# One kernel, four edits: moves of turned tiles issued by GpSimd, softmax weights turned right behind the softmax, shared buffers, and the last heads' results turned on TensorE

## The chip, the core and the metric

The kernel runs on one core of one Trainium2 chip. A core has five engines with instruction queues of their own: TensorE (PE: matrix products), VectorE (DVE), ScalarE (ACT), GpSimd (POOL) and SyncE (SP, which here only issues transfers). Each takes its instructions strictly in the order in which they stand; semaphores make one wait for another. Transfers (DMAs) are put into queues by SyncE or GpSimd and run on 16 DMA engines beside everything else. Matrix results land in PSUM, everything else lives in SBUF, both with 128 partitions.

The metric is the device time of the program in microseconds; the median of three runs before is 928.0 (927.65, 928.0 and 930.58). TensorE's clock has two levels, 2.4 and 1.2 GHz; the profile gives the granted clock of a stretch as a share of full speed.

## What is computed

A trunk of two pre-norm layers over 256 tokens of width 2048, everything in float32, weights read from HBM:

```
layer 0:  u = rms_norm(x);  [qa ka va qb kb vb gate] = u @ w_in_even        # 2048 -> 6656
  A: 8 heads of 128, 2 kv heads; q, k RMS-normalised and rotated
     ya = softmax(qa ka^T / sqrt(128)) va
  B: 8 heads; two maps of 64 each, with a linear bias on the distance
     p  = softmax(s1) - lam * softmax(s2);   yb = rms_norm(p vb) * (1 - lambda_init)
  h = x + (concat(ya, yb) * silu(gate)) @ w_out_even                          # 16 heads -> 2048
layer 1:  u = rms_norm(h);  [q k v gate] = u @ w_in_odd                       # 2048 -> 8192
  C: 16 heads of 128, three dilated windows merged into one masked, biased softmax
     h = h + (softmax(...) v * silu(gate)) @ w_out_odd
out = rms_norm(h)
```

## The kernel before

**Products.** Each float32 weight is split into a high and a low part (`hi`, `lo`), likewise each activation, and three matmuls give one product (`mm3`, lines 156 to 158). Weights come in pieces of 128 x 1024 (512 KB): `wgroup` (line 132) loads one on SyncE's queue (line 146) into one of three `raw` buffers, ScalarE makes `hi` (line 148), VectorE `lo` (line 149). A *group* below is what TensorE does with one piece: 12 matmuls of 512 columns. A projection of 512 columns (`job_t`, line 173) has eight groups. Two PSUM banks of the pool `acc` hold a job; four are there.

**Order of the work.** A scheduler works out the order of the whole program from program order, which gives priorities, and its own estimates of times. It also decides which groups of a later job fill the time in which TensorE would wait for heads. In program order the even layer has, for each of two halves g (lines 527 to 549): the queries of A, the gate, four A heads (`softmax_a`, `weighted_v`), the gate and the queries and keys of B, two pairs of B heads (`softmax_b`), the values, and the results of the pairs (`pair_b`). Then comes the output projection in four chunks of 512 columns (lines 556 to 565). `jobs_out` runs the first two chunks side by side: their groups 0 to 5 need the results y of the first twelve heads only, their groups 6 and 7 those of the last four B heads. So there are twelve groups that fill. The odd layer has four parts of gate, q, k, v and four C heads each (lines 568 to 587), then its output projection.

**Turning a tile.** Matmuls need tiles with tokens along the free axis. `turned` (line 243) transposes a 128 x 512 tile in blocks of 32 by two VectorE instructions (line 247) into a buffer `x` (two of them), and four DMAs on SyncE's queue (line 251) move the blocks to their partitions: a *move*, four issues of 64 KB each, into a buffer `pt` or `gate` (three each). 85 calls make 340 DMAs. The queries, keys, gates, the softmax weights p, the B results (line 422) and the input of the odd layer go through it. SyncE's queue carries these moves and the weight loads in one order; an issue that waits for its tile holds all that stand behind it.

**Heads.** The softmax takes a maximum (line 332), two exponentials with sums (line 335), a reciprocal and two scalings. A B head does that for two maps, with a bias from GpSimd (line 376) added on VectorE (line 371), and subtracts one from the other (line 397). The weights are turned where they are used: `weights_t` (line 343) calls `turned` and splits p into `ph` and `pl` (lines 222 and 223). `pair_b` (line 400) multiplies with the values, sums squares, takes a power on GpSimd (line 203, tile `rb`), scales (line 420) and turns the results (line 422) before they are split into y (lines 261 and 263). The maps and p live in four buffers `s` (line 341).

## Time and profile before

| | |
|---|---|
| median of 3 runs | 928.0 us (927.65 to 930.58) |
| the profiled execution's own time | 929.34 us |
| its span, first to last instruction | 927.6 us |
| mean granted TensorE clock | 0.978 |
| TensorE busy | 885.8 us, 95% |
| VectorE, ScalarE, GpSimd busy | 70%, 56%, 10% |
| DMA, mean over the span | 201 GB/s |

The profile comes from one execution. Its page gives the busy time of each engine; further views cut the span into windows, list the instructions of an engine in time order with what ended the idle time before them, group instructions by line and shape, and list transfers from issue to landing. Busy time of TensorE counts a matmul from its start to the modelled end; matmuls overlap, so their pitch, start to start, is shorter than one's own time. A short clock-down shows in PEclk, the mean of the granted clock in a stretch.

### The profile page before, as it was taken

How to read it: one execution, taken by the hardware profiler on the slowest of the kernel's cores; microseconds unless marked ns; L12 is line 12 of the kernel's file. 1: busy time of each engine (PE TensorE's matmuls, PEld its weight loads, DVE VectorE, ACT ScalarE, POOL GpSimd, SP SyncE). 2: the span in 40 equal slices, each digit the busy share in tenths (PEclk: the TensorE clock that was granted, in tenths of full speed). 3: DMA queues.
4: the chain of work that ended last, by engine and by line, in shares of the span. 5: the costliest groups of instructions: out<-in, count | busy, mean ns of one | idle time of the engine just before them, and what ended most of it. 6: DMA issues, size and time to landing. Idle time of an engine off the chain costs nothing.

```text
span 927.6 us, 12116 instructions
## 1 busy us (share of the span) xinstructions
PE 885.8 (95%) x4116; PEld 734.8 (79%) x4116; DVE 647.9 (70%) x941; ACT 522.5 (56%) x842; POOL 91.2 (10%) x61
## 2 busy tenths in 40 slices
PE   9998999999999988498999999999999999999996
PEld 7787888888878867476888888888878888887886
DVE  6687768986956798466765587558856785577663
ACT  6754656965555595244554575446645664565542
POOL 0010000210100022000000060006000510040000
PEclk9999999999999999698999999999999999999999
DMA  8866666466575555426667755775566566667653
GB/s 292 286 231 191 207 219 204 164 206 194 183 230 189 160 198 179 131 64 207 222 208 228 242 182 184 226 237 178 192 216 219 193 206 215 211 196 229 214 200 116
DMA packets 95998, 186.69 MB, mean 201 GB/s; under 512 B 10816, under 2 KB 55104, under 8 KB 95936
## 3 DMA queue, kind: packets, MB, share of 16 engines
q1 hardware_dynamic: 95616, 184.87, 61.2%
q0 software_dynamic: 320, 1.05, 0.5%
q8 instruction: 32, 0.52, 0.2%
q14 instruction: 30, 0.25, 0.1%
HBM read 161.50 MB, written 2.10 MB: 176 GB/s over the span
## 4 chain that ended last, share of the span: by engine, by line
PE 50%; DVE 16%; DMA 12%; ACT 7%; SPq 7%; issue 6%; POOL 1%; DVEq 0%; ACTq 0%; POOLq 0%
PE acc_t L157 16%; PE acc_t L158 15%; PE acc_t L156 15%; DVE lo L149 6%; SPq L251 6%; ACT hi L148 4%; DMA pt<-x 4%; DVE x L247 4%; DMA raw<-in_w_in_odd 4%; DMA raw<-in_w_in_even 2%; DMA tok<-in_x 1%; DVE nm L332 1%; DVE s L371 1%; ACT s L335 1%; DMA raw<-in_w_out_odd 1%
## 5 line engine op out<-in xcount | busy, mean ns | idle before, releaser
L149 DVE TENSOR_TENSOR lo<-raw,hi 128x1024 fp32r<-128x1024 f32 (+1 forms) x294 | 356.5, 1215 | 181.1 <-ACT hi L148 180.4
L148 ACT ACTIVATE hi<-raw 128x1024 fp32r<-128x1024 f32 (+1 forms) x294 | 308.5, 1050 | 236.4 <-PE acc_t L158 120.6
L157 PE MATMUL acc_t<-lo,u 128*128 128x512 f32 x928 | 363.3, 393 | 3.6 <-DVE lo L149 3.4
L158 PE MATMUL acc_t<-hi,u 128*128 128x512 f32 x928 | 361.5, 391 | 0.0
L156 PE MATMUL acc_t<-hi,u 128*128 128x512 f32 x928 | 330.6, 392 | 4.6 <-ACT hi L148 3.6
L157 PEld LDWEIGHTS acc_t<-lo,u 128*128 128x128 f32 x928 | 175.0, 189 | 44.4 <-DVE lo L149 8.7
L156 PEld LDWEIGHTS acc_t<-hi,u 128*128 128x128 f32 x928 | 174.2, 189 | 42.1 <-ACT hi L148 5.3
L158 PEld LDWEIGHTS acc_t<-hi,u 128*128 128x128 f32 x928 | 175.2, 189 | 34.6
L156 PE MATMUL acc_t<-hi,y 128*128 128x512 f32 (+1 forms) x256 | 93.0, 393 | 20.8 <-ACT y L261 14.0
L376 POOL TENSOR_SCALAR bias<-geo 128x512 f32<-128x512 f32 x24 | 48.7, 2029 | 551.6 <-DVE s L371 508.1
L157 PE MATMUL acc_t<-lo,y 128*128 128x512 f32 (+1 forms) x256 | 100.4, 392 | 1.1 <-DVE lo L149 1.0
L158 PE MATMUL acc_t<-hi,y 128*128 128x512 f32 (+1 forms) x256 | 97.3, 384 | 0.0
L156 PEld LDWEIGHTS acc_t<-hi,y 128*128 128x128 f32 x256 | 50.0, 197 | 31.5 <-ACT y L261 14.6
L157 PEld LDWEIGHTS acc_t<-lo,y 128*128 128x128 f32 x256 | 50.4, 197 | 11.8 <-DVE lo L149 2.9
L158 PEld LDWEIGHTS acc_t<-hi,y 128*128 128x128 f32 x256 | 49.4, 193 | 8.8
L247 DVE STREAM_TRANSPOSE x<-z 128x256 f32<-128x256 f32 x82 | 45.5, 605 | 0.6 <-DVE lo L149 0.3
L247 DVE STREAM_TRANSPOSE x<-s 128x256 f32<-128x256 f32 x72 | 41.6, 617 | 4.5 <-DMA pt<-x 3.6
L335 ACT ACTIVATE s<-s,nm 128x256 f32<-128x256 f32 x64 | 31.8, 498 | 17.8 <-DVE nm L332 17.8
L222 ACT ACTIVATE ph<-pt 128x512 fp32r<-128x512 f32 x32 | 20.2, 631 | 35.4 <-DMA pt<-x 34.9
L223 DVE TENSOR_TENSOR pl<-pt,ph 128x512 fp32r<-128x512 f32 x32 | 23.3, 729 | 12.3 <-ACT ph L222 12.2
L229 ACT ACTIVATE z<-acc_t,rstd 128x512 f32<-128x512 f32 x40 | 27.0, 676 | 4.5 <-PE acc_t L158 4.5
L378 POOL TENSOR_TENSOR bias<-bias,geo 128x512 f32<-128x512 f32 x16 | 27.7, 1731 | 1.3
(133 smaller groups left out, 661.5 us busy)
## 6 DMA issues: line engine op xcount, KB each, us to landing
raw<-in_w_in_odd SPq DMA_DIRECT2D x128, 512.0 KB, 4.2
raw<-in_w_in_even SPq DMA_DIRECT2D x102, 512.0 KB, 4.1
pt<-x SPq DMA_DIRECT2D x292, 64.0 KB, 2.2
raw<-in_w_out_even SPq DMA_DIRECT2D x32, 512.0 KB, 3.7
raw<-in_w_out_odd SPq DMA_DIRECT2D x32, 512.0 KB, 3.5
gate<-x SPq DMA_DIRECT2D x48, 64.0 KB, 2.1
tok<-in_x SPq DMA_DIRECT2D x4, 512.0 KB, 9.1
xk<-in_xt SPq DMA_DIRECT2D x6, 256.0 KB, 5.6
```

The lines of the kernel that those rows point to most:

```text
L148: A.activation(hi[:, ks], rv[:, ks], AF.Copy)
L149: splits.append(V.tensor_sub(lo[:, ks], rv[:, ks], f(hi[:, ks])))
L156: T.matmul(ps, ah, bh, start=start, stop=False)
L157: T.matmul(ps, ah, bl, start=False, stop=False)
L158: T.matmul(ps, al, bh, start=False, stop=stop)
L223: V.tensor_sub(lo, src, f(hi))
L229: A.activation(z[:, t], ps[t], AF.Copy, scale=r[:, t:t + 1])
L247: V.transpose(x[:, :, 2 * m:2 * m + 2].rearrange("p b t c -> p t b c"), src[:, :, m * P:(m + 1) * P].rearrange("p t (r b) -> p t b r", b=4))
L251: nc.sync.dma_start(dst[:, a].rearrange("p n c -> p (n c)"), x[32 * a:32 * a + 32].rearrange("r b n c -> r (b n c)"))
L335: A.activation(e[:, t], s[:, t], AF.Exp, bias=nm[:, t:t + 1], accum_out=den[:, t:t + 1])
L376: G.tensor_scalar_mul(b, geo[:, 0], -slope)
L378: G.tensor_add(b, b, geo[:, 1])
```

## The change

1. `turned` issues its four moves on GpSimd's queue (line 254 of the new kernel) instead of SyncE's. SyncE issues weight loads and little else.
2. `softmax_a`, `softmax_b` and `softmax_c` return `turned(p)`; the later `weights` only splits. The transposes and moves of p thereby follow the softmax directly in program order, and in `softmax_b` also precede the next pair's keys.
3. Buffers: `pt` and `gate` tiles come from the pool `acts` (tag `y`), whose buffers go from 16 to 22 and are shared with the y, xk and gf tiles; the `s` tiles have three buffers instead of four.
4. In the second half (g = 1) `pair_b` turns its results by four TensorE transposes with an identity matrix into a PSUM bank (`turned_pe`), instead of `turned`. The identity is made on GpSimd at the start.

Lines shift by 3 at first and by 10 or 11 behind `turned_pe` (149 is 152, 247 is 250, 251 is 254, 332 is 343).

```diff
@@ -6,6 +6,7 @@
+from concourse.masks import make_identity

@@ -100,7 +101,7 @@
     const = ctx.enter_context(tc.tile_pool(name="const", bufs=1))
     keep = ctx.enter_context(tc.tile_pool(name="keep", bufs=1))
     wpool = ctx.enter_context(tc.tile_pool(name="wpool", bufs=3))
-    acts = ctx.enter_context(tc.tile_pool(name="acts", bufs=16))
+    acts = ctx.enter_context(tc.tile_pool(name="acts", bufs=22))
     heads = ctx.enter_context(tc.tile_pool(name="heads", bufs=2))
     work = ctx.enter_context(tc.tile_pool(name="work", bufs=2))
     small = ctx.enter_context(tc.tile_pool(name="small", bufs=4))
@@ -117,6 +118,8 @@
     gcol = const.tile([P, 2 * NK + 1], F32, name="gcol")
     ones = work.tile([P, 512], F32, tag="x", name="ones", bufs=2)[:, :P]
     G.memset(ones, 1.0)
+    ident = const.tile([P, P], F32, name="ident")
+    make_identity(nc, ident)
     nhalf = const.tile([P, 8], F32, name="nhalf")
     G.memset(nhalf, -0.5)
     first = const.tile([P, 1], F32, name="first")
@@ -240,16 +243,24 @@
 
 
 
-    def turned(src, tag="pt", bufs=3):
+    def turned(src):
 
         x = work.tile([P, 4, 4, 32], F32, tag="x", name="x", bufs=2)
         for m in range(2):
             V.transpose(x[:, :, 2 * m:2 * m + 2].rearrange("p b t c -> p t b c"),
                         src[:, :, m * P:(m + 1) * P].rearrange("p t (r b) -> p t b r", b=4))
-        dst = heads.tile([P, 4, 4, 32], F32, tag=tag, name=tag, bufs=bufs)
+        dst = acts.tile([P, 4, 4, 32], F32, tag="y", name="pt")
         for a in range(4):
-            nc.sync.dma_start(dst[:, a].rearrange("p n c -> p (n c)"), x[32 * a:32 * a + 32].rearrange("r b n c -> r (b n c)"))
+            G.dma_start(dst[:, a].rearrange("p n c -> p (n c)"), x[32 * a:32 * a + 32].rearrange("r b n c -> r (b n c)"))
         return dst.rearrange("p a n c -> p n a c")
+
+    def turned_pe(src):
+
+        ps = att.tile([P, 512], F32, tag="att", name="tp").rearrange("p (n k) -> p n k", n=4)
+        for j in range(2):
+            for t in range(NT):
+                T.transpose(ps[:, 2 * j + t], src[:, t, j * P:(j + 1) * P], ident)
+        return ps.rearrange("p n (a c) -> p n a c", a=4)
 
     def quarters(ap):
 
@@ -338,18 +349,17 @@
         return rden
 
     def stile():
-        return work.tile([P, 512], F32, tag="s", name="s", bufs=4).rearrange("p (t k) -> p t k", t=NT)
-
-    def weights_t(p):
-
-        ps = turned(p)
+        return work.tile([P, 512], F32, tag="s", name="s", bufs=3).rearrange("p (t k) -> p t k", t=NT)
+
+    def weights(ps):
+
         ph = heads.tile([P, NT, S], F32R, tag="ph", name="ph")
         pl = heads.tile([P, NT, S], F32R, tag="pl", name="pl")
         split(quarters(ph), quarters(pl), ps)
         return ph, pl
 
     def weighted_v(h, p, v, vs, gate):
-        ph, pl = weights_t(p)
+        ph, pl = weights(p)
         o = bank()[:, :S]
         for kt in range(NT):
             mm3(o, v[:, kt, 0, vs], v[:, kt, 1, vs], ph[:, kt], pl[:, kt], kt == 0, kt == NT - 1)
@@ -364,7 +374,7 @@
         rden = softmax_parts(sp, p)
         for t in range(NT):
             A.activation(p[:, t], p[:, t], AF.Copy, scale=rden[:, t:t + 1])
-        return p
+        return turned(p)
 
     def biased(sp, bias):
         s = stile()
@@ -395,14 +405,14 @@
         for t in range(NT):
             A.activation(p[:, t], p[:, t], AF.Copy, scale=rd[0][:, t:t + 1])
             V.scalar_tensor_tensor(p[:, t], e2[:, t], rd[1][:, t:t + 1], p[:, t], op0=ALU.mult, op1=ALU.add)
-        return p
-
-    def pair_b(h, ps, v, zg):
+        return turned(p)
+
+    def pair_b(h, ps, v, zg, turned):
 
         os = []
         ss = small.tile([P, 8], F32, tag="ss8", name="ss4", bufs=2)[:, :2 * NT]
         for j in range(2):
-            ph, pl = weights_t(ps[j])
+            ph, pl = weights(ps[j])
             vs = slice(j * HD, j * HD + HD)
             o = bank()[:, :S].rearrange("p (t e) -> p t e", t=NT)
             for t in range(NT):
@@ -430,7 +440,7 @@
         rden = softmax_parts(p, p)
         for t in range(NT):
             A.activation(p[:, t], p[:, t], AF.Copy, scale=rden[:, t:t + 1])
-        return p
+        return turned(p)
 
 
     parts = small.tile([P, NT, 4], F32, tag="parts", name="parts", bufs=1)
@@ -463,8 +473,8 @@
-    rope = work.tile([P, NT, 2, HD], F32, tag="s", name="rope", bufs=4)
-    row = work.tile([P, 512], F32, tag="s", name="row", bufs=4)
+    rope = work.tile([P, NT, 2, HD], F32, tag="s", name="rope", bufs=3)
+    row = work.tile([P, 512], F32, tag="s", name="row", bufs=3)

@@ -530,7 +540,7 @@
         qs = [pair_t(zq, pair, "q") for pair in range(2)]
         zg = gate_t(job_t(w_even, GATE_E + c, 512, u), rh)
         for pair in range(2):
-            gate = turned(cols(zg, pair), "gate")
+            gate = turned(cols(zg, pair))
             for j in range(2):
                 p = softmax_a(qs[pair][:, :, j], k_a[:, :, g])
                 weighted_v(4 * g + 2 * pair + j, p, v_a[:, 0], slice(g * HD, g * HD + HD), gate[:, 2 * j:2 * j + 2])
@@ -546,7 +556,7 @@
                 ps.append(softmax_b(4 * g + 2 * pair + j, qs[pair][:, :, j], kh[:, :, j], kl[:, :, j]))
         evac_v(v, job_t(w_even, B_V0 + c, 512, u), rstd)
         for pair in range(2):
-            pair_b(8 + 4 * g + 2 * pair, ps[2 * pair:2 * pair + 2], v[:, pair], cols(zg, pair))
+            pair_b(8 + 4 * g + 2 * pair, ps[2 * pair:2 * pair + 2], v[:, pair], cols(zg, pair), turned_pe if g else turned)
 
 
     y_even = list(y)
@@ -571,7 +581,7 @@
         if g == 0:
             rstd, rs, rh = token_stats(parts_o, 1.0 / math.sqrt(HD))
         zg = gate_t(ps, rh)
-        gates = [turned(cols(zg, pair), "gate") for pair in range(2)]
+        gates = [turned(cols(zg, pair)) for pair in range(2)]
         zq = evac_t(job_t(w_odd, c, 512, u), rs)
         qs = [pair_t(zq, pair, "q") for pair in range(2)]
         zk = evac_t(job_t(w_odd, D + c, 512, u), rstd)
@@ -588,7 +598,7 @@
 
 
     parts = small.tile([P, NT, 5], F32, tag="parts5", name="parts5", bufs=1)
-    gf = [work.tile([P, 512], F32, tag="s", name="gf", bufs=4) for _ in range(4)]
+    gf = [acts.tile([P, 512], F32, tag="y", name="gf") for _ in range(4)]
     for c in range(4):
         G.dma_start(gf[c], final_g[c * 512:(c + 1) * 512].unsqueeze(0).to_broadcast([P, 512]))
 
```

What this does to the order of instructions is shown at three places, with the names of tiles (a number tells one tile from another).

**TensorE, the A heads of the second half.** Names: bank is the PSUM tile of a head's scores or of its weighted values, ka the keys, q the queries, va the values, ph and pl the split weights of the softmax, acc_t0 and acc_t1 the two banks of a job, u the layer's input, y a head's result. Before, behind the third head's weighted values:

```order
L157 MATMUL bank_2383<-pl_2380,va_513 128x256
L158 MATMUL bank_2383<-ph_2379,va_513 128x256
L156 MATMUL bank_2383<-ph_2379,va_513 128x256
L157 MATMUL bank_2383<-pl_2380,va_513 128x256
L158 MATMUL bank_2383<-ph_2379,va_513 128x256
L157 MATMUL acc_t0_3092<-lo_3132,u_102 128x512
L158 MATMUL acc_t0_3092<-hi_3131,u_102 128x512
L156 MATMUL acc_t0_3092<-hi_3131,u_102 128x512
L157 MATMUL acc_t0_3092<-lo_3132,u_102 128x512
L158 MATMUL acc_t0_3092<-hi_3131,u_102 128x512
```

Now, behind the second head's:

```order
L161 MATMUL bank_2339<-ph_2335,va_518 128x256
L159 MATMUL bank_2339<-ph_2335,va_518 128x256
L160 MATMUL bank_2339<-pl_2336,va_518 128x256
L161 MATMUL bank_2339<-ph_2335,va_518 128x256
L159 MATMUL acc_t0_3412<-hi_3453,y_2348 128x512
L160 MATMUL acc_t0_3412<-lo_3454,y_2348 128x512
L159 MATMUL acc_t1_3413<-hi_3453,y_2348 128x512
L160 MATMUL acc_t1_3413<-lo_3454,y_2348 128x512
L161 MATMUL acc_t0_3412<-hi_3453,y_2348 128x512
L161 MATMUL acc_t1_3413<-hi_3453,y_2348 128x512
L159 MATMUL bank_2388<-ph_2384,va_518 128x256
L335 MATMUL bank_2400<-ka_556,q_2103 128x256
```

Before, those five are followed by the matmuls of the V job (input u), some 60 of them before the next head's weighted values. Now that job is behind, and six matmuls of the output projection, with the second head's own result y_2348, stand between the second head's weighted values and the third's; the third's and fourth's are parted by six likewise. The score matmuls of the next head (bank_2400) stand behind the first weighted matmul of the head before (bank_2388).

**VectorE, the B heads of the second half.** Names: x is the buffer of a transposed tile, z the projected tile that it is taken from, s a map of scores or its softmax, nm, den and rden maximum, sum and reciprocal, kl and pl low parts, yf, y, v and bias as above. Before, around the transposes of the second pair's keys (x_3004):

```order
L247 STREAM_TRANSPOSE x_2916<-z_2912 128x2x4x32 x2
L286 TENSOR_TENSOR q_2748<-pt_2743,q_2748 64x512 x2
L247 STREAM_TRANSPOSE x_3004<-z_2912 128x2x4x32 x2
L307 SCALAR_TENSOR_TENSOR v_2915<-acc_t0_3092,rstd_506,v_2915 128x2x256
L286 TENSOR_TENSOR q_2761<-pt_2756,q_2761 64x512
L357 TENSOR_TENSOR yf_2431<-bank_2424,gate_2349 128x256
L286 TENSOR_TENSOR q_2761<-pt_2756,q_2761 64x512
L307 SCALAR_TENSOR_TENSOR v_2915<-acc_t1_3093,rstd_506,v_2915 128x2x256
L223 TENSOR_TENSOR y_2433<-yf_2431,y_2433 128x256
L297 TENSOR_TENSOR kl_2925<-pt_2919,kh_2924 64x512 x2
L371 TENSOR_TENSOR s_2941<-bank_2936,bias_2934 128x512
```

Now, around the same transposes (x_3025):

```order
L343 TENSOR_REDUCE nm_3005<-s_3003 128x2
L348 RECIPROCAL rden_3010<-den_3007 128x2
L403 TENSOR_SCALAR rden_3010<-rden_3010,nlam_491 128x2
L407 SCALAR_TENSOR_TENSOR s_2989<-s_3003,rden_3010,s_2989 128x256 x2
L250 STREAM_TRANSPOSE x_3017<-s_2989 128x2x4x32 x2
L250 STREAM_TRANSPOSE x_3025<-z_2917 128x2x4x32 x2
L226 TENSOR_TENSOR pl_3281<-pt_2977,ph_3280 128x512
L226 TENSOR_TENSOR pl_3302<-pt_3020,ph_3301 128x512
L308 TENSOR_TENSOR kl_3034<-pt_3028,kh_3033 64x512 x2
L381 TENSOR_TENSOR s_3050<-bank_3045,bias_3043 128x512
```

Before, the second pair's keys are turned right behind the first pair's, before the first pair's maps (bank_2936) are even added to their bias. Now they are turned behind the softmax of both heads of the first pair, whose weights (s_2989) are turned first, and the score maps of the second pair (bank_3045) come two splits of weights later.

**GpSimd, the same B heads.** Names: bias is the distance bias of a head, geo its source, rb the power of the squares of a pair's results, r that of the tokens. Before, all of it from the second head's bias to the token's power:

```order
L376 TENSOR_SCALAR bias_2969<-geo_323 128x512
L376 TENSOR_SCALAR bias_3022<-geo_323 128x512
L376 TENSOR_SCALAR bias_3057<-geo_323 128x512
L376 TENSOR_SCALAR bias_4644<-geo_323 128x512
L378 TENSOR_TENSOR bias_4644<-bias_4644,geo_323 128x512
L203 TENSOR_TENSOR rb_3301<-rb_3301,nhalf_86 128x4
L203 TENSOR_TENSOR rb_3384<-rb_3384,nhalf_86 128x4
L203 TENSOR_TENSOR r_4282<-r_4282,nhalf_86 128x2
```

Now the moves stand in the same queue:

```order
L386 TENSOR_SCALAR bias_3043<-geo_328 128x512
L254 DMA pt_3020<-x_3017 128x1x128 x4
L254 DMA pt_3028<-x_3025 128x1x128 x4
L386 TENSOR_SCALAR bias_3086<-geo_328 128x512
L254 DMA pt_3081<-x_3078 128x1x128 x4
L386 TENSOR_SCALAR bias_4643<-geo_328 128x512
L206 TENSOR_TENSOR rb_3322<-rb_3322,nhalf_91 128x4
L254 DMA pt_3124<-x_3121 128x1x128 x4
L388 TENSOR_TENSOR bias_4643<-bias_4643,geo_328 128x512
L206 TENSOR_TENSOR rb_3386<-rb_3386,nhalf_91 128x4
L254 DMA pt_3709<-x_3706 128x1x128 x4
```

The power rb_3322 of the first pair's results stands behind the moves of the second pair's keys (pt_3028) and of its first head (pt_3081) and behind a bias. On SyncE's queue, in turn, the moves are gone: 88 loads of the even projection's weights, 32 of its output's, 128 and 32 of the odd layer's stand there one behind the other.

## Rows read from the trace of the kernel before

**Rows 1.** page of the whole run: busy us of each engine (share of span) xinstructions.

```profile
PE 885.8 (95%) x4116; PEld 734.8 (79%) x4116; DVE 647.9 (70%) x941; ACT 522.5 (56%) x842; POOL 91.2 (10%) x61
```

**Rows 2.** busy time in stretches: us, each engine's busy us (xinstructions), PEclk, DMA, GB/s.

```profile
86.00:96.00 10.00, 7.38 (x26) 5.37 (x25) 4.92 (x7) 4.86 (x10) 0.00 (x0) 0.83 0.74 250
256.00:266.00 10.00, 7.99 (x29) 5.90 (x28) 6.14 (x9) 4.65 (x9) 0.00 (x0) 0.83 0.76 264
323.00:339.00 16.00, 12.73 (x56) 9.71 (x55) 14.50 (x24) 14.67 (x28) 3.41 (x2) 0.89 0.49 163
366.00:400.00 34.00, 19.96 (x79) 16.07 (x78) 14.44 (x30) 8.47 (x18) 1.01 (x1) 0.70 0.35 108
412.00:428.00 16.00, 9.40 (x33) 6.81 (x33) 9.57 (x22) 6.86 (x10) 0.00 (x0) 0.79 0.63 198
...
428.00:840.00 412.00, 410.18 (x1883) 340.74 (x1882) 284.92 (x371) 226.46 (x334) 55.63 (x33) 1.00 0.65 209
```

**Rows 3.** SyncE's queue in time order: start us, us, line, operation, tiles, xcount.

```profile
76.19 6.38 SPq L251 DMA_DIRECT2D pt<-x  x8
...
85.25 8.78 SPq L146 DMA_DIRECT2D raw<-in_w_in_even  x5
...
404.86 12.29 SPq L251 DMA_DIRECT2D pt<-x  x16
...
417.20 12.51 SPq L146 DMA_DIRECT2D raw<-in_w_out_even  x7
```

**Rows 4.** issues of two lines: duration ns min/median/max, first and last start.

```profile
L251 SPq DMA_DIRECT2D pt<-x x292: 542/602/1882, 57.8 to 844.9; - x146
...
L593 POOL DMA_DIRECT2D gf<-in_final_norm_g x4: 546/549/754, 830.8 to 843.6; - x4
```

**Rows 5.** costliest groups by line and shape: xcount | busy us, mean ns | idle before.

```profile
L149 DVE TENSOR_TENSOR lo<-raw,hi 128x1024 fp32r<-128x1024 f32 x290 | 353.7, 1222 | 179.6 <-ACT hi L148 179.1
...
L335 ACT ACTIVATE s<-s,nm 128x256 f32<-128x256 f32 x64 | 31.8, 498 | 17.8 <-DVE nm L332 17.8
...
L376 POOL TENSOR_SCALAR bias<-geo 128x512 f32<-128x512 f32 x24 | 48.7, 2029 | 551.6 <-DVE s L371 508.1 <-DVE rden L393 29.4 <-DVE rden L337 9.1
...
L332 DVE TENSOR_REDUCE nm<-s 128x2 f32<-128x512 f32 x32 | 21.3, 672 | 0.1
```

**Rows 6.** GpSimd in time order: one power.

```profile
385.16 1.01 POOL L203 TENSOR_TENSOR rb<-rb,nhalf 128x4 f32<-128x4 f32 x1 [20.38 <-DVE rb L202]
```

**Rows 7.** DMA issues: xcount, KB each, median us to landing.

```profile
pt<-x SPq DMA_DIRECT2D x292, 64.0 KB, 2.2
...
gf<-in_final_norm_g POOLq DMA_DIRECT2D x4, 256.0 KB, 4.8
...
row<-in_rows SPq DMA_DIRECT2D x1, 256.0 KB, 6.7
```

**Rows 8.** VectorE and ScalarE in time order, one softmax and its move.

```profile
306.54 0.68 DVE L332 TENSOR_REDUCE nm<-bank 128x2 f32<-128x512 f32 x1
...
310.76 1.16 DVE L247 STREAM_TRANSPOSE x<-s 128x256 f32<-128x256 f32 x2
...
316.00 0.63 ACT L222 ACTIVATE ph<-pt 128x512 fp32r<-128x512 f32 x1 [1.02 <-DMA pt<-x]
```

**Rows 9.** TensorE in time order: start us, us, line, matmul, xcount.

```profile
329.47 0.28 PE L388 MATMUL bank<-kh,q 128*128 128x256 f32 x1
329.58 0.28 PE L389 MATMUL bank<-kl,q 128*128 128x256 f32 x1
...
360.01 0.39 PE L156 MATMUL acc_t<-hi,y 128*128 128x512 f32 x1
360.24 0.39 PE L157 MATMUL acc_t<-lo,y 128*128 128x512 f32 x1
```

**Rows 10.** ScalarE in time order: the keys of a head pair.

```profile
324.89 0.62 ACT L295 ACTIVATE kh<-pt 64x512 fp32r<-64x512 f32 x1
...
327.48 1.28 ACT L298 ACTIVATE kl<-kl 64x512 fp32r<-64x512 f32 x2
```

## The prediction

> **What bounds the kernel now.** I read the busy line of the page first: TensorE is busy 885.8 us, 95% of the span, and no other engine is over 70% [rows 1]. So only the holes between its matmuls, and the stretches at its lower clock, are there to be won or lost. The windows show where they are [rows 2]. The reader is to see that 428 to 840, nearly half of the span, has 410.18 us of work in 412.00: 1.8 us to win in it. The five short windows hold the rest. In each I count the idle time and, for the half clock, (1 - PEclk) x busy time. 86 to 96: 2.6 + 1.3 = 3.9; 256 to 266: 2.0 + 1.4 = 3.4; 323 to 339: 3.3 + 1.4 = 4.7; 366 to 400: 14.0 + 6.0 = 20.0; 412 to 428: 6.6 + 2.0 = 8.6. Together 40.5 us.
>
> Who opens them shows in SyncE's queue [rows 3]. At 76.19 eight moves of turned tiles stand in front of the weight loads, which go on at 85.25, just before the hole at 86; the hole at 256 looks the same. At 404.86 sixteen moves wait for the results of the even projection, and seven loads of its weights behind them go only at 417.20: the hole of 412 to 428. The holes at 323 and 366 are of another kind: there the matmuls that fill are used up, and TensorE waits for the last keys and results of branch B.
>
> **GpSimd issues the moves.** In the new order SyncE holds nothing but loads, 280 in a row, so the three holes that its mixed queue opens go: 3.9 + 3.4 + 8.6 = -15.9. Nothing of the moves can stop a load after that; what is late next is the buffer of a load (three), freed by the splitting, which runs through TensorE's 412 us stretch today with 1.8 us lost [rows 2].
>
> What a move costs now: 340 issues, 85 calls of four. An issue takes 602 ns on SyncE, and 546 to 754 on GpSimd, by its four gf loads [rows 4]: equal, 4 x 0.6 = 2.4 a call, 340 x 0.6 = 204 us of a GpSimd that is busy 91.2 [rows 1]. That fits, but GpSimd's own work now stands between moves: biases at 2.03 us [rows 5] and powers at 1.01 [rows 6]. How long a 64 KB move takes from GpSimd's queue the trace doesn't show. From SyncE it is 2.2; a 256 KB row broadcast takes 4.8 from GpSimd and 6.7 from SyncE [rows 7]. From the transposes' end to the copy behind the move I read 316.00 - (310.76 + 1.16) = 4.1 [rows 8], four issues within it. Bounds for each: 2.2 instead of 4.1, if GpSimd's issues cost the chain nothing (-1.9), and 4.8 instead of 2.2 for the transfer (+2.6). I take 0, since the pair of like shape (4.8, 6.7) doesn't make GpSimd the slower path. Six moves lie on the chains below: -11 to +16.
>
> The Trainium skill, DMA: Bandwidth & Descriptors (Specifications), gives about 1 us to the first byte on GpSimd's path and 0.6 on SyncE's; by it the six moves would add an estimated 6 x 0.4 = 2.4. No row here parts the first byte from the rest, and rows 7 have the one comparable pair the other way round, so it stays out of the sum.
>
> **Transposes right behind the softmax.** This puts no more instructions on VectorE (two of 0.58 a head, [rows 8], now earlier). Their place in the order is what counts, since each now keeps its turn among maxima, adds and weight splits. And the scheduler, with other tiles and buffers, has put TensorE's work in another order; it costs more than any edit. TensorE takes its instructions as they stand, so I walk the new order with the durations of the old rows.
>
> First place, the last three A heads of g=1. Before, some 60 matmuls of the V job stand between two of their steps. Now that job is over, and between one head's weighted matmuls and the next head's stand six of the output projection. A head's chain: maximum at 306.54, copy done at 316.63 (316.00 + 0.63): 10.1 [rows 8]; six score matmuls and the first weighted one at some 0.12 [rows 9] are 0.8: 11.0 a head, 33.0 for three. In that time TensorE has 42 matmuls at 0.23 [rows 9] and 36 at 0.12: 14.0. Idle: +19.0.
>
> Second place, the last two B pairs. Before, eight groups of filling matmuls were left behind pair 0's scores. Now 23 matmuls are left, and in that order none of the output's matmuls comes until y_3335 (results of pair 0) is there. From t = 0, pair 0's scores ready: the fillers end at 23 x 0.23 = 5.3. VectorE has four adds and four maxima at 0.67, three weight splits at 1.22, four transposes at 0.58, four products at about ScalarE's 0.5 for that shape (an estimate), a wait for the last map's two exponentials, 1.0, and about 1 of small operations [rows 5, 8]: 15.4 until pair 0's second head is turned. Only behind that come pair 1's keys: +1.2 transposes, 4.1 move, and about 1 behind the four issues of that head's move: 21.7. The keys' copies take 328.76 - 324.89 = 3.9 [rows 10]: scores at 25.6. One softmax to the end of its transposes is 310.76 + 1.16 - 306.54 = 5.4, a B head adds two adds and a second maximum, 2.0: 33.0. There GpSimd issues its move (2.4), computes a bias (2.0), and only then the power that pair 0's results have waited for (1.0): 38.4. Four products and a wait for VectorE about 1.7, TensorE's four transposes and ScalarE's copy about 1.5 (estimates): y_3335 at 41.6. TensorE has had 5.3 and 56 matmuls at 0.12, 6.7: idle 29.6. Pair 1's second head is turned 4.9 later and its results come some 2 us after TensorE has used pair 0's: +2. Restarts at half clock: as in 366 to 400, which has a like hole, +6 [rows 2]. Sum +37.6.
>
> **The other edits.** Results of the last pairs turned on TensorE replace four transposes and a move of 4.1 by some 1.5, inside the 41.6 already. Three s buffers instead of four: pair 0's second head waits for its second map's buffer, inside the 15.4. Shared buffers, 22 instead of 16: the y tiles no longer turn in time with moves; I find no wait, 0, and a late one costs at most one move, 4.1. The identity is made while the first loads come: 0, at most the 2.03 of a GpSimd operation of that size [rows 5]. In the odd layer the moves have a whole job between them, 0; at its end the last heads come a little later, +1.
>
> **Sum.** Before's holes all go: -15.9 of the queue, -24.7 of 323 to 339 and 366 to 400 (that is the same place, walked anew). Added: 19.0 + 37.6 + 1 = 57.6. Net +17.0 on the profiled execution of 929.3: 946.3. The median of the runs is 928.0, 1.3 under it: 945.
>
> **Rivals.**
> *Shorter chains: faster.* The 10.1 of a head was measured while SyncE and VectorE had other things in front. With nothing in between, a head is 0.67 + 1.0 (exponentials) + 1.0 (scaling) + 1.2 + 2.2 (move) + 0.6 + 0.8 = 7.5 [rows 5, 7, 8], three are 22.5, idle 8.5. In the second place three moves give back 5.7, and splits that stand elsewhere 3.7: idle 20, with 2 + 4 behind it. Added 8.5 + 26 + 1 = 35.5 against 40.5: -5, and with the GpSimd bias done before it is needed another 2 and a little: -8, 920. For it: fewer fillers also mean fewer splits on VectorE (353.7 us of its 647.9 [rows 1, 5]) while the chain runs. Against: the order has the splits among the chain's instructions. It decides once the chains lose 17 of their 57.
> *No change, 928.* Half of that: the chains lose just those 17.
> *Moves from GpSimd are slow: worse.* +2.6 for each of six: +15.6, 961. For it: the only four transfers from GpSimd run at the very end, from 830.8 [rows 4], so the trace shows none among busy engines. Against: rows 7. It decides above 4.8 a move.
> The Trainium skill, SBUF — State Buffer (SBUF: two separate sides), says that a VectorE operation in its two-port mode keeps GpSimd from writing the descriptors of its own DMAs; an operation with two SBUF inputs, as the weight split of 1222 ns [rows 5], meets only GpSimd operations that read. If the split blocked too, a move would wait up to one of them: an estimated 6 x 1.2 = 7, inside this rival's 15.6. The four gf loads of rows 4 and 7 do not tell it.
> *The moves still hold up the loads.* SyncE's order excludes it, unless two queues share engines so that loads land late; 3.9 to 8.6 would come back, inside the forecast's range.
>
> **How the numbers follow.** Forecast, the two long chains exposed: 0.54, own range 932 to 955 (the move's bounds at half, 5 to 8 each way, and 5 for the estimates). Faster: 0.24, around 920 (908 to 926). No change: 0.08. Slow moves: 0.14, around 961. I place the range at 916 to 960: under it some 0.08, over it some 0.08. Measurements of this kernel can tell 0.3%, 2.8 us. From the cases: faster 0.24, same 0.08, slower 0.68.
>
> **What would show it.** Right: no hole at 86 and 256, loads of the output weights early; TensorE at over 95% up to the V job's end, then three stops of about 6 us in front of weighted matmuls of the last A heads, with the splitting of p (lines 225 and 226 of the new kernel) as releaser and a move behind it, and a stop of 20 us or more in front of y_3335, with GpSimd's power on its chain; the clock under 0.8 there. After it no hole until the end. Wrong: the transfer of a move at over 4.8 or under 2; the stops under 3 us (the chains are shorter); holes in the odd layer, where I charge none; TensorE waiting for raw tiles, with loads landing later than 4 us.

## The result, and the profile after

The changed kernel takes 950.2 us (949.5 to 952.6, four runs), where the kernel before took 928.3 in the same comparison: 1.0236 times as long, 95% interval 1.0210 to 1.0261. In a later comparison it was 949.9 against 934.5, ratio 1.0160 (1.0135 to 1.0186): the kernel before is slower there, the changed one is not. So ratios below are against the kernel before of the same comparison. 945 was forecast, slower.

The busy line, to be held against [rows 1]:

```profile
PE 890.5 (94%) x4124; PEld 742.3 (78%) x4124; DVE 650.4 (68%) x937; ACT 523.7 (55%) x842; POOL 257.1 (27%) x395
```

TensorE, VectorE and ScalarE have the work they had; GpSimd has 166 us more: 181 of issues, while its biases take 15 less. Then the windows with the columns of [rows 2]:

```profile
86.00:96.00 10.00, 10.00 (x47) 8.35 (x46) 7.72 (x10) 7.28 (x12) 2.16 (x4) 1.00 0.67 215
256.00:266.00 10.00, 10.00 (x46) 8.29 (x45) 8.51 (x14) 5.74 (x7) 4.48 (x6) 1.00 0.53 177
315.00:345.00 30.00, 13.93 (x49) 10.39 (x48) 14.09 (x24) 9.44 (x22) 10.81 (x21) 0.74 0.34 98
372.00:410.00 38.00, 10.90 (x58) 9.83 (x56) 23.18 (x51) 18.76 (x57) 17.87 (x25) 0.62 0.23 63
410.00:440.00 30.00, 26.46 (x97) 20.36 (x98) 14.48 (x27) 9.64 (x19) 5.42 (x9) 0.80 0.23 72
440.00:840.00 400.00, 400.00 (x1837) 333.84 (x1836) 279.00 (x367) 222.83 (x319) 126.39 (x191) 1.00 0.65 214
```

The holes at 86 and 256 are gone, and 440 to 840 has none at all. Nearly all that was lost stands in 315 to 440, where the granted clock also falls to 0.62 of 2.4 GHz behind the long stops. What TensorE waited for, in us in total, times and the longest:

```profile
PE bank L398 <- ACT kh L307: 17.6, 2, 16.9
PE bank L159 <- ACT ph L225: 13.9, 4, 5.3
PE tp L262 <- DVE s L430: 11.3, 2, 8.9
PE acc_t L159 <- ACT y L225: 4.6, 4, 1.5
```

Before, the two longest waits were for late results (y) and late weights (hi):

```profile
PE acc_t L156 <- ACT y L261: 14.0, 2, 9.1
PE acc_t L156 <- ACT hi L148: 10.1, 3, 6.6
```

Now it is the keys of the last pair (kh), the weights of the A heads (ph), and the results scaled by their power (s). The three stops at the A heads, in time order of TensorE:

```profile
318.97 0.39 PE L159 MATMUL bank<-ph,va 128*128 128x256 f32 x1 [3.14 <-ACT ph L225]
...
329.57 0.54 PE L159 MATMUL bank<-ph,va 128*128 128x256 f32 x1 [4.02 <-ACT ph L225]
...
340.45 0.58 PE L159 MATMUL bank<-ph,va 128*128 128x256 f32 x1 [5.25 <-ACT ph L225]
```

One head follows the other by 10.6 and 10.9 us. And the move: VectorE's maximum and transposes and ScalarE's copy behind them, the issues on GpSimd, and the transfers' time to landing:

```profile
331.43 0.69 DVE L343 TENSOR_REDUCE nm<-bank 128x2 f32<-128x512 f32 x1 [1.19 <-PE bank L337]
...
334.36 1.15 DVE L250 STREAM_TRANSPOSE x<-s 128x256 f32<-128x256 f32 x2 [0.41 <-ACT s L376]
```

```profile
339.77 0.63 ACT L225 ACTIVATE ph<-pt 128x512 fp32r<-128x512 f32 x1 [5.45 <-DMA pt<-x]
```

```profile
L254 POOL DMA_DIRECT2D pt<-x x332: 534/569/752, 57.9 to 882.1; - x166
```

```profile
pt<-x POOLq DMA_DIRECT2D x332, 64.0 KB, 3.3
```

From the transposes' end (335.51) to the copy it is 4.3, against 4.1 in [rows 8]; at the two A heads before it is 4.8 and 4.3. An issue is a little shorter than in [rows 4]. The median time to landing, 3.3 over the whole run, is 1.1 above that in [rows 7], but the four transfers of this move landed in 2.0 to 2.1. Last, the chain of the last B pairs on three engines:

```profile
380.15 1.14 DVE L250 STREAM_TRANSPOSE x<-s 128x256 f32<-128x256 f32 x2
381.21 1.11 DVE L250 STREAM_TRANSPOSE x<-z 128x256 f32<-128x256 f32 x2
...
398.48 1.14 DVE L250 STREAM_TRANSPOSE x<-s 128x256 f32<-128x256 f32 x2
```

```profile
399.92 2.22 POOL L254 DMA_DIRECT2D pt<-x  x4 [4.03 <-DVE x L250]
402.21 1.48 POOL L386 TENSOR_SCALAR bias<-geo 128x512 f32<-128x512 f32 x1
403.67 1.03 POOL L206 TENSOR_TENSOR rb<-rb,nhalf 128x4 f32<-128x4 f32 x1
```

```profile
389.15 0.58 PE L398 MATMUL bank<-kh,q 128*128 128x256 f32 x1 [16.92 <-ACT kh L307]
...
405.82 0.48 PE L262 MATMUL tp<-ident,s 128*128 128x128 f32 x1 [8.87 <-DVE s L430]
...
410.03 0.80 PE L159 MATMUL acc_t<-hi,y 128*128 128x512 f32 x1 [0.62 <-ACT y L272]
```

The keys (x<-z) are turned right behind the last weights (x<-s), and the power stands behind a move and a bias, as the order had it.

### The profile page after: what moved, and what is told of

It reads as the page before. It is cut to its first block, busy times and chain, and to the rows that moved or that the text cites. A ratio compares the mean times of both kernels' runs of the same rounds, so it can differ in the third digit from the quotient of the medians.

```text
span 950.8 us, 12189 instructions
## 1 busy us (share of the span) xinstructions
PE 890.5 (94%) x4124; PEld 742.3 (78%) x4124; DVE 650.4 (68%) x937; ACT 523.7 (55%) x842; POOL 257.1 (27%) x395
## 4 chain that ended last, share of the span: by engine, by line
PE 56%; DVE 2%; ACT 2%; issue 2%; DMA 2%; POOL 1%; POOLq 0%; DVEq 0%; ACTq 0%
PE acc_t L159 18%; PE acc_t L160 17%; PE acc_t L161 17%; DMA pt<-x 2%; POOL pt L254 1%; PE bank L160 1%; ACT s L346 1%; PE bank L161 1%; PE bank L159 1%; DVE x L250 0%; PE bank L337 0%; PE bank L336 0%; PE bank L335 0%; ACT hi L151 0%; DVE s L381 0%
## 5 line engine op out<-in xcount | busy, mean ns | idle before, releaser
L254 POOL DMA_DIRECT2D pt<-x x332 | 180.9, 574 | 402.1 <-issue 135.1
L160 PEld LDWEIGHTS acc_t<-lo,u 128*128 128x128 f32 x928 | 174.1, 188 | 37.6 <-DVE lo L152 2.4
L386 POOL TENSOR_SCALAR bias<-geo 128x512 f32<-128x512 f32 x24 | 40.3, 1681 | 166.1 <-DVE s L381 160.6
L160 PEld LDWEIGHTS acc_t<-lo,y 128*128 128x128 f32 x256 | 50.6, 198 | 10.1 <-DVE lo L152 1.1
L226 DVE TENSOR_TENSOR pl<-pt,ph 128x512 fp32r<-128x512 f32 x32 | 21.7, 677 | 13.5 <-ACT ph L225 13.5
```

Of the source, the lines that this page charges most:

```text
L160: T.matmul(ps, ah, bl, start=False, stop=False)
L226: V.tensor_sub(lo, src, f(hi))
L254: G.dma_start(dst[:, a].rearrange("p n c -> p (n c)"), x[32 * a:32 * a + 32].rearrange("r b n c -> r (b n c)"))
L386: G.tensor_scalar_mul(b, geo[:, 0], -slope)
```

## Experiments

Two theories at the start. *Order*: the order of TensorE, made for GpSimd's queue, spends the filling matmuls too soon. *Transfers*: moves from GpSimd are themselves slow. A third came out of the runs.

**Undo the queue.** `turned` in the changed kernel, else untouched:

```diff
-            G.dma_start(dst[:, a]...
+            nc.sync.dma_start(dst[:, a]...
```

> The changed kernel with its moves issued by SyncE again; all else of it stays. Theory order (the changed kernel lost its time because the order made for GpSimd's queue uses up the filling matmuls before the heads' chains): the three stops in front of weighted matmuls of A heads in the second half (14 us, with some 60 matmuls of a projection between heads again) go, the stop in front of the second pair's scores (17 us) shrinks by the 12 more filling matmuls, 3 us; the three holes of the mixed queue (16 us) come back in part. About 940 us (934 to 946). Theory transfers (GpSimd's moves themselves are the cost, 3.3 us to landing against 2.2): only the six moves on the chains give back 6 x 1.1 = 7 us and the queue's 16 us come back: about 959 us.

934.1 us, ratio 0.9984 (0.9963 to 1.0006): like the kernel before. In microseconds this is the lower end of the first theory's range and far off the other; the range was made beside a kernel before of 928, and by the ratio the result lies under it (934 is 1.006 of 928). The A heads' stops are gone; the keys' stop is not:

```profile
PE bank L398 <- ACT kh L307: 16.9, 2, 16.2
PE tp L262 <- DVE s L430: 7.1, 2, 3.7
PE acc_t L159 <- ACT hi L151: 6.6, 5, 1.9
```

**The queue alone**, the reverse edit in the kernel before.

> The kernel before with its moves issued by GpSimd and nothing else changed. Theory order: the three holes of SyncE's queue go (-16), but the A heads of the second half end behind the V job (34, then 6 filling matmuls between their steps: stops of some 1.5 and 7 us), and 70 instead of some 158 filling matmuls are left behind the first pair's scores, 20 us less cover for the last B heads: about 942 us (934 to 950). Theory transfers: order is harmless, -16 + 7 = about 920 us.

938.1 us, ratio 1.0025 (1.0009 to 1.0040). The stops at A heads and results come as in the first theory:

```profile
PE acc_t L156 <- ACT y L261: 19.6, 2, 10.3
PE bank L156 <- ACT ph L222: 16.9, 4, 7.4
```

The time lies between the two theories: made from 928, their forecasts are ratios of 1.015 (1.006 to 1.024) and 0.991. So each half of the change by itself is worth nothing or nearly so, and both together cost 1.6 to 2.4%: they are not to be added.

**Turn the weights late again**, in the changed kernel:

```diff
-        return turned(p)          # softmax_a, _b, _c
+        return p
-    def weights(ps):
+    def weights(p):
+        ps = turned(p)
```

> The changed kernel with the softmax weights turned where they are used, as before the change; moves from GpSimd, shared buffers and the turning on TensorE stay. Theory order: the A heads' stops stay as they are (6 filling matmuls between the last of them, as with the change), and the second pair's keys no longer stand behind the first pair's weights on VectorE and GpSimd: the stop of 17 us in front of its scores shrinks, what is gained there is lost in part in front of the results, since the weights are turned later: 938 to 948 us, 943 the likeliest. Rival (the early turn costs nothing by itself): 950 us.

949.9 us, ratio 1.0163 (1.0135 to 1.0190), the changed kernel's time: the rival was right. The keys' stop of 17 us goes, and 14 come up in front of the weights, against the 13.9 above:

```profile
PE bank L159 <- ACT ph L225: 27.7, 7, 7.6
```

**GpSimd for the moves that stand before late loads only**, in the kernel before:

```diff
-    k_a = pair_t(tok_heads(ps_kv, 1, 2), 0, "ka", 1)
+    k_a = pair_t(tok_heads(ps_kv, 1, 2), 0, "ka", 1, G)
-        qs = [pair_t(zq, pair, "q") for pair in range(2)]      # A's queries
+        qs = [pair_t(zq, pair, "q", eng=G) for pair in range(2)]
-            xk = turned(tok[:, :, k * P:k * P + S])
+            xk = turned(tok[:, :, k * P:k * P + S], eng=G)
```

> The kernel before with only some moves on GpSimd: those of A's queries and keys and of the odd layer's input, the ones that stand in front of late weight loads. TensorE's order keeps 60 matmuls of a projection between the steps of the A heads and 38 to 61 filling matmuls in front of each weighted product of the last B heads. Theory order: the holes at 86, 256 and 412 us go, nothing is lost for them: -12 to -16, about 914 us (910 to 919). Theory transfers: the same moves cost 1.1 us more each where they are waited for, four places: about 919 us. If the holes had another cause than the mixed queue: 928 us.

919.4 us, ratio 0.9825 (0.9787 to 0.9863): 16 us off, the first theory's -12 to -16. That 919 is also the other theory's number is chance, since that was made from 928, a ratio of 0.990. 13 of the 85 calls held up the loads.

**The changed kernel itself, and its fillers in another sequence.**

> The changed kernel itself, beside the kernel before and the next three on one chip, since the chips differ: ratio to the kernel before 1.015 to 1.026; stops at the same places, 53 us of them in sum.

949.9 us, 1.0160 as above, the stops where they were (52 us in sum).

```diff
-        for kgs in (range(6), range(6, 8)):
+        for kgs in (early, range(6, 8)):
...
-    for i, cs, ps in jobs_out(w_oe, CHUNKS_E, y_even):
+    for i, cs, ps in jobs_out(w_oe, CHUNKS_E, y_even, (0, 1, 4, 5, 2, 3)):
```

> The changed kernel with one line different: the output projection takes its weight groups in the order 0, 1, 4, 5, 2, 3 and not 0 to 5, so that those which need the A heads of the second half come last. No transfer, buffer or softmax changes. TensorE's order gets 54, 66 and 12 filling matmuls between the steps of the last A heads instead of 30, 6 and 6, and none instead of 23 in front of the second pair's scores. Theory order: the first two stops at the A heads go, the third stays at 5 us, the first pair's scores come some 6 us earlier, and so does all behind them: 6 to 8 us off, ratio to the changed kernel 0.992 to 0.994. Theory transfers: no transfer is changed, 1.000.

945.6 us, ratio to the kernel before 1.0115 (1.0087 to 1.0142): 4.3 off instead of 6 to 8. Two of the A heads' stops went (waits for ph 7.1 instead of 13.9), and the waits for keys grew from 17.6 to 25.8. No transfer was touched, so TensorE's order is worth some 4 us by itself; the rest of the gain was given back at the next stop.

**Results turned by moves** in the changed kernel (`turned` in place of `turned_pe if g else turned`).

> The changed kernel with the last B heads' results turned by VectorE and GpSimd's moves, as before the change, and not on TensorE. Two transposes of 0.58 and a move of 4.1 come instead of 1.25 (TensorE's transposes) and 0.56 on each of the two chains to the results: +3.4 for the first pair, and up to as much for the second: 3 to 7 us slower than the changed kernel, ratio 1.004 to 1.007. Rival (TensorE's transposes gain nothing, since other work hides the moves): 1.000.

949.3 us, ratio to the kernel before 1.0166 (1.0135 to 1.0198): no difference, the rival was right. The first pair's results are used from 413.9 on instead of 410.0, but the second pair's, which end the stage, from 423.4 on instead of 423.7 (423.1 in the changed kernel's second trace).

**Tie TensorE's order**, first in the second half, by edges from the projections' matmuls to the A heads' scores; first in the changed kernel, then in the kernel before with all moves on GpSimd:

```diff
+            n = -1 if n0 is None else (n0 + kg - 11) // 5
+            with tc.issue_after(scored[4 + min(n, 3)].ins) if n >= 0 else nullcontext():
```

> The changed kernel, all moves from GpSimd, with only TensorE's order pinned in the second half: the groups of the four projections behind the A heads' queries are tied behind the A heads' scores, five groups to a head, so that 60 matmuls stand between the steps of the A heads again as before the change (with the change 71, 30, 6, 6 were there, all of them late). Theory order: the stops at the A heads (14 us in the changed kernel's trace, and 3 of half clock behind them) go, and 35 instead of 23 filling matmuls stand in front of the second pair's scores, 3 us off that stop: 930 us on the scale where the changed kernel has 950, ratio to it 0.977 to 0.985. Theory transfers (GpSimd's queue brings the queries and weights too late for the old places): TensorE stops in front of the heads' new places for about as long, 945 to 950.

947.6 us, ratio to the kernel before 1.0123 (1.0083 to 1.0164), near the other theory's 945 to 950. The A heads' stops went, and one came in front of their first scores:

```profile
PE bank L339 <- ACT q L227: 24.7, 1, 24.7
PE bank L403 <- ACT kh L309: 14.8, 2, 14.0
```

> The kernel before with all moves on GpSimd and the same pinning of TensorE's order. Theory order: the two stops at A heads in the kernel with GpSimd's moves alone (5.0 and 4.4 us and 4 small ones, 13 in sum) go, and some 37 more filling matmuls, 8 us, stand in front of the last B heads' products, where 32 us of stops were: 938 - 13 - 8 = about 917 us (912 to 924) where that kernel has 938. Theory transfers: 932 to 938.

933.5 us, ratio 0.9973 (0.9953 to 0.9994): a gain of 5 on the untied kernel and not of 21, with the same new stop at the queries, 14.4.

**Four s buffers** again, 21 shared ones:

> The changed kernel with four s buffers as before the change, and 21 shared ones instead of 22 to make room. TensorE's order is the same, so this is the buffer alone: in the changed kernel the second map of the first pair's second head (VectorE's add at 374.80) waits until the first head's weights are turned (373.68 to 374.85). With a fourth buffer it comes some 3 us earlier, and the keys behind it too: the stop of 17 us in front of the second pair's scores falls to some 14: 947 where the changed kernel has 950, ratio 0.996 to 0.998. Rival (VectorE is full there anyway): 1.000.

947.3 us, ratio 1.0118 (1.0078 to 1.0159), the longest wait for keys 15.8 against 16.9, and the waits for the scaled results 9.6 in sum against 11.3. The trace shows the forecast's size, but the ratio's interval overlaps the changed kernel's 1.0135 to 1.0186, so the times can't tell it from none.

**Tie it from the first half on** (`PINS` gives the number of groups in front of each head event, `at` the events):

```diff
+PINS = (28, 34, 39, 44, 53, 54, 55, 56, 60, 64, 71, 72, 84, 89, 94, 99)
+            n = sum(n0 + kg >= first for first in PINS) - 1
+            with tc.issue_after(at[n].ins) if n >= 0 else nullcontext():
```

> The changed kernel with all its edits and all moves from GpSimd; only TensorE's order is tied, now from the first half on: the groups of the even projections are tied behind the head events at the places that they have before the change (A scores behind 28, 34, 39 and 44 groups, the first pairs' scores behind 53 to 56, their weighted values behind 60 to 72). In the changed kernel the same events stand behind 72 to 84 matmuls a head instead of 60, and the second half's first A head behind 1171 of the 1248 projection matmuls; here it stands behind 926 (993 before the change), with 72 to 77 between the heads, and 59 instead of 23 filling matmuls stand in front of the last pair's scores. Theory order from the first half on (the scheduler's spacing, not any engine, holds the heads back): no stop of weight at the pinned places, the A heads' stops (14 us and 3 of half clock) go, the stop of 17 us falls by 36 x 0.23 = 8: 925 us (916 to 934) where the changed kernel has 950, ratio to it 0.964 to 0.983. Rival (VectorE, ScalarE and GpSimd hold the heads back with their queues): TensorE stops in front of scores at the pinned places, 942 to 950, ratio 0.991 to 1.000.

947.6 us, ratio 1.0126 (1.0080 to 1.0172): the rival. The A heads of the first half ran at 85.6, 102.7, 117.8 and 132.8 without a stop, so no engine needs the 17.8 us from head to head that the changed kernel's order gives them. Then TensorE stopped for keys, in both halves:

```profile
PE bank L404 <- ACT kh L310: 35.9, 6, 14.6
PE tp L265 <- DVE s L438: 11.6, 2, 9.2
```

In the first half one sees the second pair's keys (x<-z) behind the first pair's weights (x<-s) on VectorE, and their moves on GpSimd:

```profile
182.99 1.15 DVE L253 STREAM_TRANSPOSE x<-s 128x256 f32<-128x256 f32 x2
184.08 1.09 DVE L253 STREAM_TRANSPOSE x<-z 128x256 f32<-128x256 f32 x2
```

```profile
184.72 4.39 POOL L257 DMA_DIRECT2D pt<-x  x8 [1.82 <-ACT ph L228]
```

It is the pattern of 380 to 389 again, uncovered. So the first theory falls in the form that it had: tying TensorE's order did not shorten the stops' sum (pauses between the starts of matmuls of over 0.6 us beyond the pitch: 52 us in the changed kernel, 55 and 54 in the two tied ones). The powers of the last two pairs start at 403.7 and 419.6 in the changed kernel, at 402.1 and 419.3, and at 403.2 and 418.9, in the tied ones: tying TensorE's order changed where it stops, and hardly when the stage ends. What makes the chains so long is not shown. The ties leave the order on VectorE, ScalarE and GpSimd to the scheduler, and from 177 to 192 in this last run, while TensorE waits, none of the three is full (busy for 9.7, 6.2 and 9.0 of 15 us). So their order and the time of moves from GpSimd both remain as causes; undoing the queue (sp_moves) changes both at once, and no run parts them. How late the heads come, by the start of each event's first matmul or power in us:

| | before | sp_moves | gp_moves_only | late_turn | changed_again |
|---|---|---|---|---|---|
| first half, A head 1 and 4 | 82.6, 134.5 | 83.3, 133.3 | 85.8, 141.3 | 85.2, 140.7 | 85.3, 140.8 |
| first half, B, first pair | 161.5 | 166.7 | 174.7 | 183.6 | 183.7 |
| last power of the first half | 226.5 | 234.0 | 241.3 | 256.7 | 255.8 |
| second half, A head 1 | 254.8 | 261.7 | 275.6 | 291.0 | 289.5 |

Up to there TensorE is hardly ever idle in any of them, so the table shows where TensorE's order puts the heads, and not yet what they need. The last tied kernel shows that they need part of it: its last power of the first half comes at 228.4 and its first A head of the second at 263.7, and to be so early TensorE stopped for 24 us in front of the first half's keys.

The lag at the last row is 7 us with the other edits alone, 21 with the queue alone and 35 with both. One reading, for which there is no run of its own: it is paid out of a fixed stock of work that waits for no head, and when that is used up, the second half shows the rest as stops. That would also say why the edits don't add, and why late or early turning is the same: the last power of the first half comes at 256 with either. From 241 (gp_moves_only) to 256 (late_turn) the queue is the same. With four s buffers that power comes at 254.9, with the results turned by moves at 255.7, so the shared pool is left for this step, by exclusion only.

**A selection**: the 13 calls from GpSimd, `turned_pe` for the last results, gate buffers two instead of three; else the kernel before.

> A selection, from the kernel before: GpSimd issues the moves of A's queries and keys and of the odd layer's input alone, and the last B heads' results turn on TensorE; weights turn where they are used, SyncE issues all other moves, gate buffers two instead of three to make room. Theory order: the mixed queue's holes stay away as in the kernel with those moves alone (ratio 0.9825), and the two stops in front of the last results, 4.5 and 9.1 us there, lose 3.4 each: ratio to the kernel before 0.972 to 0.979. If the results' turning is hidden anyway: 0.982.

902.1 us, ratio to the kernel before 0.9654 (0.9627 to 0.9680), and 5% under the changed kernel. That is 6 us under the forecast's lower end. Its busy line and the window to be held against that of [rows 2]:

```profile
PE 877.4 (98%) x4124; PEld 730.2 (81%) x4124; DVE 644.5 (72%) x937; ACT 520.9 (58%) x842; POOL 121.7 (14%) x115
```

```profile
366.00:400.00 34.00, 31.67 (x139) 25.01 (x138) 24.01 (x44) 17.46 (x34) 9.74 (x17) 1.00 0.57 181
```

Both of the stops that turning on TensorE was to shorten are all but gone (one wait of 1.8 us for y is left), and with them the half clock, which the forecast had left out: the clock was 0.70 in that window before, and with the 13 calls alone. There the turning pays, since there its chain was the last.

## Why the prediction was right, step by step

- *The queue's holes go, -15.9*: right. The windows at 86 and 256 are full, and 13 calls on GpSimd alone gave 16 us.
- *A move costs the same*: right on the chains, 4.3 to 4.8 against 4.1. The slow rival decided above 4.8 for the transfer alone; the one shown landed in 2.0 to 2.1.
- *First place, +19.0*: the sum is right, in part by luck. 315 to 345 has 16.1 idle and 0.26 x 13.9 = 3.6 of half clock, 19.7; the forecast was 19.0 of idle time, and charged no half clock here. The three stops were 3.1, 4.0 and 5.3 us, where about 6 each was forecast. The period of 11.0 was 10.6 to 10.9, and that too is two errors that cancel: from maximum to copy done it was 9.0 (331.43 to 340.40) and not 10.1, and the matmuls in front of the maximum took 1.6 to 1.9, at half clock for the most part, and not 0.8.
- *Second place, +37.6*: 372 to 440 has 30.6 idle, where 31.6 was forecast, and 4.1 + 5.3 of half clock, where 6 was: 40.0. Step by step from the first pair's scores (366.9): second head turned at 14.4 (forecast 15.4), keys split from 20.9 (21.7), next head turned at 32.7 (33.0), power done at 37.8 (38.4), first matmul with its result at 43.1 (41.6). The chain and its size are right. What was to show it came otherwise: instead of one stop of 20 us or more in front of the results there were 16.9 in front of the second pair's scores and 8.9 in front of the results, as two links of the same chain.
- *End of the odd layer, +1*: mis-sized. The last 81 us have 11.5 idle and 2.8 of half clock against 8.4 and 1.5: +4.4. With the half clock of the second place this is most of what the time lies over the forecast: 64.1 are added instead of 57.6, and the profiled spans differ by 23.2 instead of 17.0.
- *It costs more than any edit that TensorE's order is new*: right as an account of this trace, not borne out as the cause. Tied back, TensorE stopped elsewhere for as long. The chains were taken as given from the second half on; that the heads come late from the first half on, under full cover, was not in the text, nor that the parts don't add.
- *TensorE's turning inside the sum* (1.5 for 5.3): no gain shown in this kernel. It is a gain where that chain ends last.
- *The faster rival* (7.5 a head, 6.7 of it from maximum to copy): the chains did get shorter with less work in front, by 1.1 of its 3.4 us a head, and half clock took that back.

## What to carry to other kernels

Look at when each stage starts, and not only at where the engine stops: work that waits for nothing can cover a chain that gets longer, and what it no longer covers shows up later. That is how the table above reads in this kernel. Price a change of queue by the moves that hold something up: 13 of 85 calls gained 16 us, and all 85 gained nothing; what the other 72 cost, and by which engine, was not taken apart. And tie the order before blaming it: if the stops move and their sum stays, that engine's order was not the main cause.

## What the runs showed of the hardware that was not expected

The same program's time differs between comparisons, which ran on several chips, by under 1%, and not alike for all kernels: the kernel before had medians of 928.3 and 934.5 to 936.7, the changed one 950.2 and 949.9.

A 64 KB move lands in 3.3 us from GpSimd and 2.2 from SyncE (medians), but most of that goes with what runs beside it. In the changed kernel's trace the 41 moves with a weight load under way for less than half of the time from issue to landing landed in 2.1 us, the 271 with a load under way for nearly all of it in 3.6. In the kernel before it is 2.1 (178 moves) and 2.6 (76). The Trainium skill, DMA: Bandwidth & Descriptors (Specifications), gives about 1 us to the first byte on GpSimd's path and 0.6 on SyncE's, an estimated 0.4 between them. No row parts the first byte from the rest; of the landings as a whole the traces show no difference without loads, and one of 1.0 beside them.

No lengthening by VectorE's weight splits is seen: beside loads, the 155 moves with a split running for over half of the first 1.2 us behind the start of their issue landed in 3.1 us, the 39 with next to none in 4.0.
